# A Trainium2 decoder trunk: the experts' buffers open before the routing, six weight slots come through POOL's queue into h's place, and ten unused products stand on TensorE

## The chip, the cores and the metric

The kernel runs on one core of a Trainium2 chip. The metric is device time in microseconds (us) of one execution; the time of a kernel is the median of its timed runs. One further execution is recorded by the hardware profiler; all rows below come from it.

The engines in the profile are PE (TensorE's products), PEld (its weight loads), DVE (VectorE), ACT (ScalarE), POOL (GpSimd) and SP (SyncE, which here only issues transfers). Each engine runs its instructions in the order in which the program wrote them.

## The reference, cut to what matters

Two layers over 512 tokens of 1024 features. Layer 0 is an mLSTM mixer and a dense SwiGLU, layer 1 an HGRN2 mixer and a top-2-of-8 expert SwiGLU. All inputs are float32.

```python
def rmsnorm(x, w):
    x32 = x.astype(jnp.float32)
    y = x32 * lax.rsqrt(jnp.mean(x32 * x32, axis=-1, keepdims=True) + EPS)
    return (y * w.astype(jnp.float32)).astype(x.dtype)

def swiglu(t, wg, wu, wd):
    return (jax.nn.silu(t @ wg) * (t @ wu)) @ wd

def moe_swiglu(h, router_w, wg, wu, wd):
    ...
    logits = (t @ router_w).astype(jnp.float32)
    top_logits, top_idx = lax.top_k(logits, TOP_K)
    top_w = jax.nn.softmax(top_logits, axis=-1)
    gates = jnp.einsum('tk,tke->te', top_w, jax.nn.one_hot(top_idx, N_EXPERTS, dtype=jnp.float32)).astype(h.dtype)
    for e in range(N_EXPERTS):
        y = y + gates[:, e:e + 1] * swiglu(t, wg[e], wu[e], wd[e])
...
    for layer in range(DEPTH):
        ...
        hn = rmsnorm(x, norm1_w[layer]) * (1 + scale1) + shift1
        y = mlstm_mixer(hn, ...)  or  hgrn2_mixer(hn, ...)
        x = x + gate1 * y
        hn = rmsnorm(x, norm2_w[layer]) * (1 + scale2) + shift2
        y = swiglu(hn, ...)  or  moe_swiglu(hn, ...)
        x = x + gate2 * y
    return rmsnorm(x, final_norm_w)
```

## The kernel before, in words

**Products.** The residual stream is held feature-major: eight tiles `x[k]` of 128 features by 512 tokens. A float32 product is three products of fp32r halves (`hi`, `lo` of the activations, `whi`, `wlo` of the weights: hi by whi, lo by whi, hi by wlo); the experts use two. So every projection is a long row of 128x512 products on PE, k tile by k tile.

**Weights.** All weights are stored as *slots* of 128x1024 float32 (512 KB). The class `Weights` (lines 160 to 255) walks one list, `plan`, of entries of two slots or one. `load` issues an entry's transfer on SP's queue into a buffer of the pool `raw` (two buffers of two slots); `want` lets ACT make `whi` of a slot (a copy to fp32r), `low` lets DVE make `wlo` (the difference). Split slots live in a pool of five and are made three ahead of the one that PE reads. A raw buffer is free when its last `wlo` is made, and only then is the next entry's transfer issued. In the expert phase a second pool, `rawm`, doubles the raw buffers; it is opened after the routing. Its first entries (`raw70`, `raw71`, ...) belong to expert 0. During the start (`ada_first`, line 506), entries 2 and 3 go to a pool `rawf`, and the transfers of the conditioning weights `ad0` to `ad7` (1 MB each) stand between them on SP's queue.

**The norm** (`norm`, line 597). The sum of squares of each token comes from two float32 products `ms<-sq,mean`; ACT turns it into `rs` with two activations; then, for each of eight k tiles, DVE makes `u`, ACT makes `hi` and DVE makes `lo`, and PE runs that tile's products (`group_first`). Of the three norms that go through this function, the first has other work passed in (`before`); the ones ahead of the dense SwiGLU (products `f_in`) and ahead of the HGRN2 projection (products `h_first`) have none.

**Routing and experts.** The last projection of HGRN2 (`h_out`) runs interleaved with `pre_route` (line 1288): residual tiles `xr0` to `xr7` come back from DRAM on POOL's queue, PE makes the logits (`lgt`, `lps`) and transposes of the tokens (`xt`). Then `route` (line 1351) has DVE and ACT work out the two best experts and the place of each token in its expert's list (`mask_b`, `rps`, `pick`), while PE waits. `experts` (line 1563) then takes the eight experts one after the other: PE gathers the expert's tokens into columns (`xT<-pick,xt`, 152 at most), ACT copies them (`xm`), PE makes gate and up products (`gu`), ACT and DVE make `h` (one tile of 2x152 for each of 11 blocks, a buffer each), PE makes the down products (`yd`). Expert e's first three blocks of gate and up (`EARLY`) stand ahead of the down products of expert e-1. What does not fit in an expert's 152 places goes through a branch, `overflow`.

**Names in rows.** A helper records every operation, so that nearly all rows carry its line, L317; the tile names tell them apart. Tiles shown without their number (`raw`, `xr`) stand for all of that name.

Of the kernel before, what the change touches and what calls it, by code (L numbers as in the profile page):

```python
# [152 lines left out]
def moe_order():  # L153

    for e in range(NE + 1):
        if e < NE:
            yield from ((e * MB // 8 + 2 * f, 2) for f in range(EARLY))
        if e:
            base = (e - 1) * MB // 8 + 2 * ET
            yield from ((base + i, min(2, ET - i)) for i in range(0, ET, 2))  # L160
        if e < NE:
            yield from ((e * MB // 8 + 2 * f, 2) for f in range(EARLY, ET))


class Weights:
# [4 lines left out]
    def __init__(self, nc, raw, split, bufs, plan, ahead, loads):  # L170
        self.nc, self.raw, self.split, self.bufs, self.plan = nc, raw, split, bufs, plan
        self.ahead, self.loads, self.early = ahead, loads, {}
# [5 lines left out]
    def load(self, n):  # L178
        while self.next_load < min(n, len(self.plan)):
            src, s0, cnt = self.plan[self.next_load]  # L180
            pool = self.early.get(self.next_load) or self.raw[self.next_load % len(self.raw)]
            t = pool.tile([P, 2, 1024], F32, name=f"raw{self.next_load}", tag="raw")
            self.nc.sync.dma_start(t[:, 0:cnt], src[s0:s0 + cnt].rearrange("s p c -> p s c"))
            for i in range(cnt):
                self.raws[self.loaded] = (t[:, i], self.next_load + (i == cnt - 1))
                self.loaded += 1
            self.next_load += 1

    def want(self, slot):

        nc, left = self.nc, []
        while self.next_slot < min(slot + 1, self.n_slots, self.freed + self.bufs):
            s = self.next_slot
            while s not in self.raws:
                self.load(self.next_load + 1)
# [9 lines left out]
    def low(self, left):  # L205
        for lo, r, hi, i in left:
            self.nc.vector.tensor_sub(lo, r, hi.bitcast(F32))
            self.load(i + 1 + self.loads)
# [179 lines left out]
class Kernel:  # L388
    def __init__(self, nc, tc, ctx, a, dbg):
# [10 lines left out]
        self.W = Weights(nc, [pool("raw", 2)], pool("split", 5), 5, plan, 3, 1)  # L400
# [91 lines left out]


# [12 lines left out]
    def ada_first(self, pool):  # L506
# [22 lines left out]
        for d in range(6):  # L529
            if d % 2 == 0:  # L530
                self.W.load(d // 2 + 1)
            load(d)
        self.W.load(4)
# [63 lines left out]
    def norm(self, l, i, before=()):  # L597
# [3 lines left out]
        for s, t in enumerate(self.ssq):  # L601
            nc.tensor.matmul(ms, self.mean, t, start=s == 0, stop=s == 1)
        rs = self.nrm.tile([P, T], F32, name="rs", tag="rs", bufs=1)
# [114 lines left out]
    def mlstm(self):  # L718
# [3 lines left out]
        with ExitStack() as ctx:  # L722
# [5 lines left out]
            with tc.tile_pool(name="adf", bufs=6) as adf, tc.tile_pool(name="rawf", bufs=2) as rawf:  # L728
                self.W.early = {2: rawf, 3: rawf}
                a0 = self.ada_first(adf)  # L730
# [747 lines left out]
    def moe(self, out, stop):  # L1478
        nc, tc = self.nc, self.tc
        V, S = nc.vector, nc.scalar  # L1480
        with ExitStack() as ctx:
# [9 lines left out]
            nc.gpsimd.memset(self.one_b, 1.0)  # L1491
            lps = self.ps("lps", (P, NC, NE))
# [7 lines left out]
            for _ in self.side:  # L1500
                pass
            pick, rest, *slots = self.route(rp, lps, xt)
            with ExitStack() as ctx:
                pools = [ctx.enter_context(tc.tile_pool(name=n, bufs=2)) for n in ("xe", "he", "wk", "rawm")]
                self.W.raw.append(pools.pop())
                self.W.loads = 3
                g, r, n_over = self.experts(*pools, xt, pick, lambda: rest(*slots))
# [55 lines left out]
    def experts(self, xp, hp, wk, xt, pick, rest):  # L1563
# [4 lines left out]
        xs, hs, ys, rows = {}, {}, {}, {}  # L1568
# [326 lines left out]
```

## Time and profile before

| | |
|---|---|
| time, median of 3 runs | 1565.16 us (1563.8 to 1567.88) |
| time of the profiled execution | 1567.31 us |
| its span in the trace | 1565.5 us |
| PE busy | 1492.9 us, 95% |
| DVE busy | 1088.3 us, 70% |
| ACT busy | 844.6 us, 54% |
| POOL busy | 138.8 us, 9% |
| mean granted TensorE clock | 0.975 |

The profiled execution is 1.8 us longer than its span and 2.15 us above the median of the timed runs. A busy share is a mean over stages: PE is at 99 to 100% in most of them, so its waits stand in few places, and the rows below are from these places. The granted clock is 1.00 at 2.4 GHz and 0.50 at 1.2 GHz; a stretch between has both.

### The profile page before, as it was taken

The numbers are of one execution on the slowest core, as the hardware profiler recorded it, in microseconds if no ns is written. First come the engines' busy times: TensorE is split into PE (matmuls) and PEld (weight loads), VectorE is DVE, ScalarE is ACT, GpSimd is POOL, SyncE is SP. The second block draws the span as 40 slices with busy tenths as digits, with TensorE's granted clock in tenths as the row PEclk, the third lists the DMA queues.
The fourth block names the chain that finished last, engine by engine and source line by source line (L and its number), as shares of the span: only waits on it lengthen the run. The fifth ranks groups of instructions, "written<-read, shape, count | busy, mean of one in ns | idle before, by whom it ended". The sixth has DMA issues, their size and how long they took to land.

```text
span 1565.5 us, 23553 instructions
## 1 busy us (share of the span) xinstructions
PE 1492.9 (95%) x8935; PEld 1312.3 (84%) x8935; DVE 1088.3 (70%) x1991; ACT 844.6 (54%) x1561; POOL 138.8 (9%) x209
## 2 busy tenths in 40 slices
PE   4989999999999999999999998999999999999996
PEld 3867776888888888688888875999999999999994
DVE  6785874655445555585977744787877878788796
ACT  5466433423212322364656543687776868777663
POOL 0041000000000000310000010501010010100061
PEclk8999999999999999999999999999999999999997
DMA  9462551355455553543102132788787887878782
GB/s 375 162 193 77 189 195 60 140 210 188 164 186 184 193 192 118 192 145 108 54 28 81 55 105 108 257 299 302 250 286 269 276 275 260 300 258 272 267 315 91
DMA packets 80854, 300.47 MB, mean 192 GB/s; under 512 B 8036, under 2 KB 8084, under 8 KB 79712
## 3 DMA queue, kind: packets, MB, share of 16 engines
q1 hardware_dynamic: 69424, 266.36, 48.4%
q0 software_dynamic: 11312, 32.56, 6.3%
q8 instruction: 72, 1.18, 0.3%
q14 instruction: 46, 0.38, 0.1%
HBM read 280.78 MB, written 18.09 MB: 191 GB/s over the span
## 4 chain that ended last, share of the span: by engine, by line
PE 84%; DVE 6%; ACT 4%; DMA 4%; issue 1%; POOL 0%; DVEq 0%; SPq 0%; ACTq 0%
PE gu L317 20%; PE yd L317 11%; PE fd L317 8%; PE fgp L317 7%; PE fup L317 7%; PE hh L317 4%; PE al L317 3%; PE hv L317 3%; PE h_out L317 3%; PE m_g L317 3%; PE m_out L317 2%; PE hg L317 2%; PE h_first L317 2%; PE f_in L317 1%; PE o L317 1%; DMA ar<-in_ada 1%
## 5 line engine op out<-in xcount | busy, mean ns | idle before, releaser
L317 DVE TENSOR_TENSOR wlo<-raw,whi 128x1024 fp32r<-128x1024 f32 x403 | 489.8, 1222 | 107.1 <-ACT whi L317 105.0
L317 ACT ACTIVATE whi<-raw 128x1024 fp32r<-128x1024 f32 x403 | 421.9, 1054 | 183.1 <-DMA raw<-in_w 40.3
L317 PE MATMUL gu<-x,whi 128*128 128x304 f32 x1408 | 358.6, 344 | 1.5 <-DVE x L317 1.5
L317 PE MATMUL gu<-x,wlo 128*128 128x152 f32 x1408 | 327.8, 233 | 0.0
L317 PEld LDWEIGHTS gu<-x,wlo 128*128 128x128 f32 x1408 | 269.1, 191 | 0.0
L317 PEld LDWEIGHTS gu<-x,whi 128*128 128x128 f32 x1408 | 264.4, 188 | 1.9 <-DVE x L317 1.9
L317 PE MATMUL yd<-h,whi 128*128 128x304 f32 x704 | 183.2, 348 | 2.7 <-DVE h L317 2.7
L317 PE MATMUL yd<-h,wlo 128*128 128x152 f32 x704 | 164.6, 234 | 0.0
L317 PEld LDWEIGHTS yd<-h,whi 128*128 128x128 f32 x704 | 133.3, 189 | 3.1 <-DVE h L317 3.1
L317 PEld LDWEIGHTS yd<-h,wlo 128*128 128x128 f32 x704 | 135.6, 193 | 0.0
L317 DVE SCALAR_TENSOR_TENSOR ar<-ar,cond 128x1024 f32<-128x1024 f32 x80 | 99.5, 1246 | 3.0 <-DMA ar<-in_ada 2.9
L317 ACT ACTIVATE fhi<-fg 128x512 fp32r<-128x512 f32 x22 | 13.9, 633 | 114.3 <-DVE fg L317 114.3
L317 DVE TENSOR_TENSOR fg<-fg,fup 128x512 f32<-128x512 f32 x20 | 13.8, 688 | 82.6 <-PE fup L317 82.6
L317 PE MATMUL fd<-fhi,whi 128*128 128x512 f32 x176 | 69.6, 396 | 0.0
L317 PE MATMUL fd<-flo,whi 128*128 128x512 f32 x176 | 69.6, 396 | 0.0
L317 PE MATMUL fd<-fhi,wlo 128*128 128x512 f32 x176 | 69.6, 396 | 0.0
L317 ACT ACTIVATE t<-gu 128x152 f32<-128x152 f32 x176 | 47.4, 289 | 32.3 <-PE gu L317 32.3
L317 PE MATMUL fgp<-lo,whi 128*128 128x512 f32 x160 | 62.3, 389 | 0.0
L317 PE MATMUL fgp<-hi,whi 128*128 128x512 f32 x160 | 62.2, 389 | 0.0
L317 PE MATMUL fgp<-hi,wlo 128*128 128x512 f32 x160 | 62.2, 389 | 0.0
L317 PE MATMUL fup<-hi,whi 128*128 128x512 f32 x160 | 62.2, 389 | 0.0
L317 PE MATMUL fup<-lo,whi 128*128 128x512 f32 x160 | 62.2, 389 | 0.0
(407 smaller groups left out, 2996.8 us busy)
## 6 DMA issues: line engine op xcount, KB each, us to landing
raw<-in_moe SPq DMA_DIRECT2D x128, 1024.0 KB, 5.2
raw<-in_w SPq DMA_DIRECT2D x69, 1024.0 KB, 5.0
ar<-in_ada SPq DMA_DIRECT2D x80, 512.0 KB, 4.1
ad<-in_ada SPq DMA_DIRECT2D x8, 1024.0 KB, 17.3
XG<-zero POOLq DMA_DIRECT2D x18, 256.0 KB, 6.4
xr<-XG POOLq DMA_DIRECT2D x28, 152.0 KB, 6.3
raw<-in_moe SPq DMA_DIRECT2D x8, 512.0 KB, 4.0
Y<-yt POOLq DMA_DIRECT2D x14, 256.0 KB, 3.7
```

The source lines that it names most:

```text
L317: r = f(*args, **kw)
```

## The change

Four things are changed.

1. `norm` issues three unused products behind `ms` where it has no other work passed in, that is in two of the norms. They multiply the same two operands as `ms` into a bank that nobody reads.
2. Four of the same products stand between `pre_route` and `route`.
3. The pools of the experts open ahead of `pre_route`, and `rawm` joins the raw pools there. The first six slots of expert 0 become six entries of one slot (`raw70` to `raw75`), are issued on POOL's queue at once, and land in the six buffers `hb` (128x1024 each) that `h` will use later; three tiles of `h` now share one `hb`. The later entries (`raw76` and up) go to `raw` and `rawm` on SP's queue. `load` now issues whenever a raw pool holds fewer than two entries.
4. At the start, entries 2 and 3 are fetched into `rawf` by name, and entry 4 stands ahead of `ad6` and `ad7` on SP's queue.

The diff, cut:

```diff
 def moe_order():
...
-        if e < NE:
+        if e == 0:
+            yield from ((s, 1) for s in range(2 * EARLY))
+        elif e < NE:
             yield from ((e * MB // 8 + 2 * f, 2) for f in range(EARLY))
...
+    def room(self, pool):
+        self.raw.append((pool, []))
+
+    def fetch(self, n, pool, queue, tag="raw"):
+        src, s0, cnt = self.plan[n]
+        t = pool.tile([P, 2 if tag == "raw" else cnt, 1024], F32, name=f"raw{n}", tag=tag,
+                      **({} if tag == "raw" else {"bufs": 2 * EARLY}))
+        queue.dma_start(t[:, 0:cnt], src[s0:s0 + cnt].rearrange("s p c -> p s c"))
+        self.early[n] = t
+
+    def load(self, n, done=0):
+        for _, held in self.raw:
+            held[:] = [x for x in held if x >= done]
         while self.next_load < min(n, len(self.plan)):
-            src, s0, cnt = self.plan[self.next_load]
-            pool = self.early.get(self.next_load) or self.raw[self.next_load % len(self.raw)]
...
+            m = self.next_load
+            if m not in self.early:
+                pools = [x for x in self.raw if len(x[1]) < 2]
+                if not pools:
+                    return
+                pools[0][1].append(m)
+                self.fetch(m, pools[0][0], self.nc.sync)
+            t, cnt = self.early.pop(m), self.plan[m][2]
...
     def low(self, left):
         for lo, r, hi, i in left:
             self.nc.vector.tensor_sub(lo, r, hi.bitcast(F32))
-            self.load(i + 1 + self.loads)
+            self.load(len(self.plan), i)
...
+    def warm(self, n, t):
+        ps = self.ps("warm")
+        for _ in range(n):
+            self.nc.tensor.matmul(ps, self.mean, t, start=True, stop=True)
...
         for d in range(6):
-            if d % 2 == 0:
+            if d == 4:
+                self.W.fetch(2, raw, nc.sync)
+            elif d % 2 == 0:
                 self.W.load(d // 2 + 1)
             load(d)
+        self.W.fetch(3, raw, nc.sync)
         self.W.load(4)
...
             nc.tensor.matmul(ms, self.mean, t, start=s == 0, stop=s == 1)
+        if not before:
+            self.warm(3, self.ssq[0])
         rs = self.nrm.tile([P, T], F32, name="rs", tag="rs", bufs=1)
...
             nc.gpsimd.memset(self.one_b, 1.0)
+            experts = ctx.enter_context(ExitStack())
+            pools = [experts.enter_context(tc.tile_pool(name=n, bufs=2)) for n in ("xe", "he", "wk", "rawm")]
+            self.W.room(pools.pop())
+            for n in range(2 * EARLY):
+                self.W.fetch(self.n_dense + n, pools[1], nc.gpsimd, "hb")
...
+            self.warm(4, self.ssq[0])
             pick, rest, *slots = self.route(rp, lps, xt)
-            with ExitStack() as ctx:
-                pools = [ctx.enter_context(tc.tile_pool(name=n, bufs=2)) for n in ("xe", "he", "wk", "rawm")]
-                self.W.raw.append(pools.pop())
-                self.W.loads = 3
-                g, r, n_over = self.experts(*pools, xt, pick, lambda: rest(*slots))
+            g, r, n_over = self.experts(*pools, xt, pick, lambda: rest(*slots))
+            experts.close()
...
-            h = hs[e, f] = hp.tile([P, 2, CAP], F32R, name=f"h{e}{f}", tag="h", bufs=ET + EARLY + 2)
+            n = e * ET + f
+            if n % 3 == 0:
+                hb[0] = hp.tile([P, 1024], F32R, name=f"hb{n}", tag="hb", bufs=2 * EARLY)
+            h = hs[e, f] = hb[0][:, n % 3 * 2 * CAP:(n % 3 + 1) * 2 * CAP].rearrange("p (s r) -> p s r", s=2)
```

In the changed kernel the helper's line is L337. On PE, at the norm ahead of the dense SwiGLU, stood before (`m_out` is the mLSTM's output projection):

```order
L317 MATMUL m_out_1952<-yhih_1849,wlo_1961 128x512
L317 MATMUL ms<-sq,mean 128x512 x2
L317 MATMUL f_in_2111<-hi_2107,whi_1988 128x512
L317 MATMUL f_in_2111<-lo_2109,whi_1988 128x512
L317 MATMUL f_in_2111<-hi_2107,wlo_1989 128x512
```

and stands now:

```order
L337 MATMUL m_out_1952<-yhih_1849,wlo_1961 128x512
L337 MATMUL ms<-sq,mean 128x512 x2
L337 MATMUL warm<-sq,mean 128x512 x3
L337 MATMUL f_in_2115<-hi_2111,whi_1988 128x512
L337 MATMUL f_in_2115<-lo_2113,whi_1988 128x512
L337 MATMUL f_in_2115<-hi_2111,wlo_1989 128x512
```

Three products have come between the sum of squares and the first product of the projection; ahead of HGRN2 it is the same with `h_first`.

On PE, in the routing, the changed kernel has this between the last transpose of `pre_route` and the first product of `route`; before, the row of `warm` is not there and the rest stands in the same order:

```order
L337 MATMUL xt_7322<-cst_c,xr_7146 128x128
L337 MATMUL warm<-sq,mean 128x512 x4
L337 LDWEIGHTS bef
L337 MATMUL rps<-mask_b,bef 128x32
L337 LDWEIGHTS one_b
L337 MATMUL rps<-mask_b,one_b 128x24
```

The four products stand ahead of `rps`, the product that `route` waits for.

On POOL, ahead of `pre_route`, stood before (`cst_r` and `fw` are constants, `bef` and `one_b` the routing's matrices):

```order
L1261 DMA xr5_7053<-X_83 128x512
L417 DMA cst_r_7073<-in_const_r 128x280
L1486 DMA fw_7075<-in_fnw 128x1024
L1489 CAST bef_7079<-cst_r_7073 128x128
L1491 MEMSET one_b_7081 128x128
L1261 DMA xr6_7088<-X_83 128x512
L1261 DMA xr7_7110<-X_83 128x512
```

and stands now:

```order
L1521 MEMSET one_b_7089 128x128
L189 DMA raw70_7103<-in_moe 128x1024
L189 DMA raw71_7105<-in_moe 128x1024
L189 DMA raw72_7107<-in_moe 128x1024
L189 DMA raw73_7109<-in_moe 128x1024
L189 DMA raw74_7111<-in_moe 128x1024
L189 DMA raw75_7113<-in_moe 128x1024
L1291 DMA xr6_7120<-X_83 128x512
L1291 DMA xr7_7146<-X_83 128x512
```

Six transfers of 512 KB have come ahead of the loads of `xr6` and `xr7`. On SP's queue the entries of the last HGRN2 weights were followed by expert 0's pairs:

```order
L183 DMA raw68_6924<-in_w 128x2x1024
L183 DMA raw69_7032<-in_w 128x1024
L183 DMA raw70_7144<-in_moe 128x2x1024
L183 DMA raw71_7174<-in_moe 128x2x1024
L183 DMA raw72_7273<-in_moe 128x2x1024
L183 DMA raw73_7560<-in_moe 128x2x1024
```

and are followed now by later ones:

```order
L189 DMA raw68_6932<-in_w 128x2x1024
L189 DMA raw69_7040<-in_w 128x1024
L189 DMA raw76_7123<-in_moe 128x2x1024
L189 DMA raw77_7125<-in_moe 128x2x1024
L189 DMA raw78_7180<-in_moe 128x2x1024
L189 DMA raw79_7210<-in_moe 128x2x1024
```

So SP's queue is six slots further on at the same place. At the program's start SP's queue now has `raw4` directly behind `raw3`, ahead of `ad6` and `ad7`; before, it stood directly behind `ad7`.

## Rows read from the trace of the kernel before

**Rows 1.** The page's head and its sections 1 and 4: span; busy time of each engine, share of the span and instructions; the chain that ended last, by engine.

```profile
span 1565.5 us, 23553 instructions
...
PE 1492.9 (95%) x8935; PEld 1312.3 (84%) x8935; DVE 1088.3 (70%) x1991; ACT 844.6 (54%) x1561; POOL 138.8 (9%) x209
...
PE 84%; DVE 6%; ACT 4%; DMA 4%; issue 1%; POOL 0%; DVEq 0%; SPq 0%; ACTq 0%
```

**Rows 2.** Stretches of 2 us at the first of the two norms (the one ahead of the dense SwiGLU): the stretch, its length, busy time and instructions of PE, PEld, DVE, ACT and POOL, granted TensorE clock (1.00 is 2.4 GHz, 0.50 is 1.2 GHz), mean busy share of the DMA engines, GB/s.

```profile
270.00:272.00 2.00, 0.00 (x0) 0.00 (x0) 0.75 (x1) 1.15 (x3) 0.00 (x0) 1.00 0.00 0
272.00:274.00 2.00, 1.30 (x5) 0.86 (x6) 1.61 (x2) 1.31 (x2) 0.00 (x0) 1.00 0.00 0
274.00:276.00 2.00, 2.00 (x6) 1.59 (x5) 1.21 (x3) 0.73 (x1) 0.00 (x0) 0.52 0.31 39
276.00:278.00 2.00, 2.00 (x7) 1.58 (x6) 1.21 (x3) 0.82 (x2) 0.00 (x0) 0.63 0.95 387
```

**Rows 3.** The timeline there: start, length, engine, line, operation and tiles; in square brackets the engine's idle time ahead of it and who ended it. `lo` in the fourth row belongs to the last of eight k tiles.

```profile
268.31 1.12 PE L317 MATMUL ms<-sq,mean 128*128 128x512 f32 x2 [0.33 <-ACT sq L317]
...
272.41 0.50 PE L317 MATMUL f_in<-hi,whi 128*128 128x512 f32 x1 [2.98 <-ACT hi L317]
...
273.20 0.50 PE L317 MATMUL f_in<-lo,whi 128*128 128x512 f32 x1 [0.28 <-DVE lo L317]
...
292.39 0.75 DVE L317 SCALAR_TENSOR_TENSOR lo<-u,mod,hi 128x512 fp32r<-128x512 f32 x1 [0.79 <-ACT hi L317]
...
293.98 0.39 PE L317 MATMUL f_in<-lo,whi 128*128 128x512 f32 x1
```

**Rows 4.** Stretches of 2 us at the second norm (ahead of the HGRN2 projection), columns as in Rows 2.

```profile
640.00:642.00 2.00, 0.15 (x1) 0.00 (x0) 0.43 (x1) 1.32 (x2) 0.00 (x0) 1.00 0.99 363
642.00:644.00 2.00, 0.87 (x2) 0.37 (x2) 1.21 (x3) 1.64 (x2) 0.00 (x0) 0.68 0.31 121
...
648.00:650.00 2.00, 2.00 (x7) 1.60 (x6) 1.34 (x2) 1.57 (x2) 0.00 (x0) 0.62 0.65 266
```

**Rows 5.** The timeline at the second norm, columns as in Rows 3; `lo` is again that of the last k tile.

```profile
639.03 1.12 PE L317 MATMUL ms<-sq,mean 128*128 128x512 f32 x2 [0.71 <-ACT sq L317]
...
643.13 0.80 PE L317 MATMUL h_first<-hi,whi 128*128 128x512 f32 x1 [2.98 <-ACT hi L317]
...
663.10 0.75 DVE L317 SCALAR_TENSOR_TENSOR lo<-u,mod,hi 128x512 fp32r<-128x512 f32 x1 [0.79 <-ACT hi L317]
...
665.73 0.39 PE L317 MATMUL h_first<-lo,whi 128*128 128x512 f32 x1
```

**Rows 6.** Stretches of 0.5 us of PE alone in the routing: the stretch, its length, PE busy time and instructions, granted clock, DMA share, GB/s.

```profile
973.50:974.00 0.50, 0.00 (x0) 0.80 0.00 0
...
984.00:984.50 0.50, 0.50 (x6) 0.96 0.00 0
```

**Rows 7.** The timeline of the routing and of the first gather of expert 0, columns as in Rows 3 (a product of float32 operands is two records).

```profile
972.84 0.63 PE L317 MATMUL xt<-cst_c,xr 128*128 128x128 f32 x4
...
977.75 0.18 PE L317 MATMUL rps<-mask_b,bef 128*128 128x32 bf16 x1 [4.28 <-DVE mask_b L317]
...
978.68 11.15 PE L317 MATMUL xT<-pick,xt 128*128 128x152 f32 x64 [0.68 <-DVE pick L317]
```

**Rows 8.** The chain that ended last, in order of time, in the same place: start, length, engine, tile and line, number of records.

```profile
978.68 9.09 PE xT L317 x48
...
987.80 1.23 ACT xm L317 x3
...
992.29 6.74 PE gu L317 x52
...
1038.49 10.74 PE gu L317 x84
```

**Rows 9.** The timeline at the program's start, PE alone: two products of the same operands as the unused ones, 128x512 in float32, four records.

```profile
14.29 3.78 PE L317 MATMUL ms<-sq,mean 128*128 128x512 f32 x4 [14.29 <-DVE sq L317]
```

**Rows 10.** Who waited for whom on ACT between 985 and 1040 us: in total, times, longest.

```profile
ACT whi L317 <- DMA raw<-in_moe: 6.8, 5, 2.0
```

**Rows 11.** Stretches of the expert phase, columns as in Rows 2.

```profile
1000.00:1030.00 30.00, 30.00 (x248) 30.00 (x247) 25.10 (x53) 20.78 (x45) 8.52 (x14) 1.00 1.02 371
...
1036.00:1038.00 2.00, 1.93 (x16) 1.75 (x15) 1.89 (x6) 2.00 (x5) 0.00 (x0) 1.00 0.50 107
1038.00:1040.00 2.00, 1.51 (x12) 1.51 (x12) 2.00 (x6) 1.79 (x6) 0.00 (x0) 1.00 1.03 422
1040.00:1500.00 460.00, 460.00 (x3741) 459.94 (x3741) 370.80 (x651) 345.60 (x667) 42.62 (x59) 1.00 0.81 275
```

**Rows 12.** The timeline of POOL, ACT and DVE in the last projection of HGRN2, columns as in Rows 3.

```profile
929.26 1.07 POOL L1261 DMA_DIRECT2D xr<-X  x2
...
947.43 2.00 ACT L317 ACTIVATE whi<-raw 128x1024 fp32r<-128x1024 f32 x2 [5.96 <-DMA raw<-in_moe]
...
951.33 0.60 ACT L317 ACTIVATE xt<-xt 128x512 f32<-128x512 f32 x1 [1.90 <-PE xt L317]
...
963.42 0.75 DVE L317 SCALAR_TENSOR_TENSOR xr<-h_out,mod,xr 128x512 f32<-128x512 f32 x1 [0.95 <-PE h_out L317]
```

**Rows 13.** Stretches of 5 us there, columns as in Rows 2.

```profile
925.00:930.00 5.00, 5.00 (x23) 4.13 (x23) 1.11 (x2) 1.58 (x2) 1.74 (x6) 1.00 0.70 274
930.00:935.00 5.00, 5.00 (x23) 4.13 (x22) 0.69 (x2) 0.00 (x0) 0.41 (x2) 1.00 0.33 105
935.00:940.00 5.00, 5.00 (x23) 4.13 (x22) 3.45 (x6) 2.02 (x4) 0.00 (x0) 1.00 0.01 3
940.00:945.00 5.00, 5.00 (x24) 4.14 (x23) 2.96 (x3) 1.46 (x2) 0.00 (x0) 1.00 0.22 70
```

**Rows 14.** The timeline of the program's start: issues of the SP queue, and the first DVE product that reads the last of these loads (the second of its pair follows it).

```profile
21.33 3.82 SPq L519 DMA_DIRECT2D ad<-in_ada  x2
...
25.62 6.17 SPq L183 DMA_DIRECT2D raw<-in_w  x2
...
50.94 1.21 DVE L317 SCALAR_TENSOR_TENSOR ad<-ad,cond 128x1024 f32<-128x1024 f32 x1
```

More of the change, by code (lines that the diff above doesn't have):

```diff
@@ L165, with __init__ @@
 class Weights:
-    def __init__(self, nc, raw, split, bufs, plan, ahead, loads):
-        self.nc, self.raw, self.split, self.bufs, self.plan = nc, raw, split, bufs, plan
-        self.ahead, self.loads, self.early = ahead, loads, {}
+    def __init__(self, nc, raw, split, bufs, plan, ahead):
+        self.nc, self.split, self.bufs, self.plan = nc, split, bufs, plan
+        self.ahead, self.early, self.raw = ahead, {}, []
+        self.room(raw)
         self.freed, self.used, self.left = 0, None, []
@@ L176, in __init__ @@
         self.n_slots = sum(c for _, _, c in plan)
-    def load(self, n):
-        while self.next_load < min(n, len(self.plan)):
-            src, s0, cnt = self.plan[self.next_load]
-            pool = self.early.get(self.next_load) or self.raw[self.next_load % len(self.raw)]
-            t = pool.tile([P, 2, 1024], F32, name=f"raw{self.next_load}", tag="raw")
-            self.nc.sync.dma_start(t[:, 0:cnt], src[s0:s0 + cnt].rearrange("s p c -> p s c"))
+    def room(self, pool):
[9 more added lines that the diff above has]
+            held[:] = [x for x in held if x >= done]
+        while self.next_load < min(n, len(self.plan)):
+            m = self.next_load
[6 more added lines that the diff above has]
+            t, cnt = self.early.pop(m), self.plan[m][2]
             for i in range(cnt):
-                self.raws[self.loaded] = (t[:, i], self.next_load + (i == cnt - 1))
+                self.raws[self.loaded] = (t[:, i], m + (i == cnt - 1))
                 self.loaded += 1
@@ L193, in want @@
             s = self.next_slot
-            while s not in self.raws:
-                self.load(self.next_load + 1)
+            assert s in self.raws
             r, i = self.raws.pop(s)
@@ L399, in __init__ @@
         plan += [(a["moe"], i, n) for i, n in moe_order()]
-        self.W = Weights(nc, [pool("raw", 2)], pool("split", 5), 5, plan, 3, 1)
+        self.W = Weights(nc, pool("raw", 2), pool("split", 5), 5, plan, 3)
         self.dram = pool("dram", 1, space=DRAM)
@@ L504, in bias, with ada_first @@
         return self.V(f"ab{l}").rearrange("p (j d) -> p j d", j=6)[:, j]
-    def ada_first(self, pool):
+    def ada_first(self, pool, raw):
         nc = self.nc
@@ L728, in mlstm @@
             with tc.tile_pool(name="adf", bufs=6) as adf, tc.tile_pool(name="rawf", bufs=2) as rawf:
-                self.W.early = {2: rawf, 3: rawf}
-                a0 = self.ada_first(adf)
+                a0 = self.ada_first(adf, rawf)
                 S.activation(self.cond, self.cond, AF.Silu)
@@ L1567, in experts @@
         R2, HC = CAP - P, CAP // 2
-        xs, hs, ys, rows = {}, {}, {}, {}
+        xs, hs, ys, rows, hb = {}, {}, {}, {}, [None]
         def fetch(e):
```

## The prediction

> **What bounds the kernel now.** I read the page's head first: PE is busy for 1492.9 of 1565.5 us and carries 84% of the chain that ended last [rows 1]. A long stretch of the expert phase has no gap at all, 460.00 us busy of 460.00 [rows 11]. So nothing that another engine does faster counts there; time can be won only where PE waits or where it runs at half clock. Next I read the granted clock in short stretches. At 0.50 PE has half its pace (1.2 instead of 2.4 GHz). Three of the stretches at half clock lie where this change works: behind the first norm (0.52 and 0.63 in the two stretches from 274 to 278) [rows 2], behind the second (0.68 from 642, 0.62 still in 648 to 650) [rows 4], and in the routing, where it falls between 973.5 and 974.0 and is back at 984.0 to 984.5 [rows 6]. Last I read the timeline in each place, to see who supplies PE there. The reader is to see that each fall stands beside a wait of PE: 2.98 us for ACT's first hi at each norm [rows 3, 5], 4.28 us for mask_b in the routing [rows 7].
>
> **The first norm (A).** Added: three products of the kind of ms. One such product (two records) is 1.12 us as the trace has it at full clock [rows 3], about 0.95 when they follow each other, since two of them took 3.78 at half clock, 1.89 each [rows 9]. Three take 2.8 to 3.4. They start where ms ends, 268.31 + 1.12 = 269.43, and end at 272.3 to 272.8; the first f_in product went at 272.41. So they fill the wait, and may be 0 to 0.4 us late. If the clock then stays up, 3.5 us at half (274.0 to 277.5, estimated from the stretches) would give back up to 1.7 us. But the eight k tiles come from DVE and ACT, which do not run faster for it: the last lo starts at 292.39 and takes 0.75, so its product could go at 293.2, a few hundredths behind its end. It went at 293.98; the one of the first tile, at 273.20, had waited 0.28 for its lo, so the pace is DVE's wherever PE is quick. The supply leaves 0.8 us, and hides a late warm product too. **A = 0.8**, ends 0 and 1.7; I take the supply's end, since its row is in this place.
>
> **The second norm (B).** The same three products, from 639.03 + 1.12 = 640.15 to 643.0 to 643.5, against 643.13 before [rows 5]. Half clock lasted from about 642.7 to 649.5 (estimated from the stretches), worth up to 3.4. The last lo starts at 663.10 and takes 0.75, its product could go at 663.9 and went at 665.73. **B = 1.8**, ends 0 and 3.4.
>
> **The routing (C).** xT started at 978.68 and ran at half clock until 984.04; these 5.36 us would be 2.68 at full clock. They lie on the path: the chain goes xT 9.09 us, xm at 987.80, gu at 992.29 [rows 8]. Against it stand the four products, which are ahead of rps. They start when the last xt ends, 972.84 + 0.63 = 973.47, and rps went at 977.75 [rows 7]. All at full clock, 3.8 us, they end at 977.3 and cost nothing. All at half, 7.56 us, they end at 981.0 and rps is 3.3 late. The row says that the clock fell within 0.5 us of the end of the small transposes [rows 6], ahead of any length of waiting, so I expect part of the four to be slow: two at each clock end at 973.47 + 5.68 = 979.15, 1.4 late; if only the first 1.8 are slow, 1.2. With 1.3, **C = 2.68 - 1.3 = 1.4**, ends -0.6 and 2.7.
>
> The Trainium skill, "TensorE: Matmul & The Clock Gate", Part 1, says that half clock is the default state and that activity has to come first to release it. By that rule the four products would be the ones to pay for it, all at half, with C = -0.6. The trace agrees as far as that xT itself ran slow for 5.36 us before the clock came back [rows 6, 7].
>
> **The start of the experts (D).** Between 985 and 1040 ACT waited 6.8 us in five waits for raw entries [rows 10], the DMA engines were full for 30 us at 371 GB/s, and PE lost 0.07 + 0.49 us in 1036 to 1040 [rows 11], ahead of the gu group at 1038.49 [rows 8]. Now six slots land before the routing, and four pairs follow in raw and rawm, 14 slots against four before. This wait goes. **D = 0.6**, ends 0 and 0.8 (a quicker stretch of gu products by then). What is late next is PE itself, since it is full from there on.
>
> **Edits that I cost at nothing.** Six fetches on POOL stand ahead of xr6 and xr7: an issue is 1.07 / 2 = 0.54 us [rows 12], so the two come 3.2 us later, issued near 932.5. The first reader that matters, DVE's xr, runs at 963.42 [rows 12]; 20 us of cover or more. The fetches and the first two pairs are 5.2 MB; at 371 GB/s some 14 us, from 929 to 943, when the DMA share was 0.33 and 0.01 [rows 13]. The engine that waits for them is ACT, in order, for the first whi; before, it waited for the same weights until 947.43, and what stands behind it, xt at 951.33, waited for PE anyway [rows 12]. Packing h adds no instruction, and frees a buffer by threes. At the start raw4 (1 MB, 2.8 us at 371 GB/s) delays ad6 and ad7 by about that; their issues began at 21.33 and the last DVE product that needs them ran at 50.94 [rows 14], with 2 MB to land in between. If this cover were thin, it would cost up to 2.8.
>
> **The sum.** A + B + C + D = 0.8 + 1.8 + 1.4 + 0.6 = 4.6. Against the profiled execution that is 1567.3 - 4.6 = 1562.7. The median of the timed runs is 1565.16, which gives 1560.6. Timed runs lie 4.1 us apart, as much as my sum; a run that was shorter may have had less half clock to win back. I therefore take a little less than the whole sum: **1561.2**, a gain of 4.0.
>
> **Rivals.**
>
> *More comes back.* All four routing products run at full clock (C = 2.7), and at the first norm the projection gains more than the supply bound (A up to 1.7, since DVE and ACT also split weights there that wait for buffers which PE frees). Sum 5.9 to 6.8: about 1558.8. For it: PE comes to the routing from a projection at clock 1.00 [rows 13]. Against: the clock fell within 0.5 us of PE's last transpose, so it was not the long wait that brought it down.
>
> *Less comes back.* Either the unused products do not hold the clock in the norms, and only C + D = 2.0 is left, 1563.2 (that the change does not do what it says); or the four in the routing run at half throughout, A + B + C + D = 2.6, 1562.6. For the second: xT ran at half for 5.36 us while PE was working. Against the first: nothing in PE waits is left there for a fall to stand beside.
>
> *Slower: ACT is held by the fetches.* The whi of raw70 is queued on ACT ahead of xt (951.33), on which the routing depends. If raw70 lands after 951.3, all behind it on ACT moves, and PE with it. Eating the sum takes a landing after 951.3 + 4.6 = 955.9, and slower by 0.3% after 960.6: then about 1570. From 932.5 that is 28 us for 5.2 MB, under 190 GB/s, where the trace has 371 at full share [rows 11] and idle engines just there [rows 13]; and raw70 is the first of the six.
>
> The Trainium skill, "Trainium Kernel Development and Optimization", Key Constraints, says that transfers of SP's, ACT's and POOL's queues share 16 DMA engines and interleave. So a second queue would buy order and issue time, no bandwidth. No row of before has both queues full at once.
>
> **How the numbers follow.** About 0.3% (4.7 us) is what a measurement of this kernel can tell from no change; the border lies at 1560.5. My forecast, chance 0.60, sits beside it: 0.25 on the faster side, 0.35 within. More comes back: 0.20, all faster. Less: 0.15, all within (0.08 for the first kind, 0.07 for the second). Slower: 0.05. That makes 0.45 faster, 0.50 within 0.3%, 0.05 slower. The range: down to 1557.4 (below the second case by its A and B ends), up to 1563.6 (just above the third case); what is left out is the slow case, the far ends of B and C, and an unseen spread of the median.
>
> **What the changed profile would show.** Right: clock 1.00 through both norms, and PE's lo products right behind the last lo (A, B); xT at 1.00 from its first product, 64 records in some 8.5 us instead of 11.15, with rps 1 to 1.5 us behind its mask_b (C); raw70 to raw75 landing between 930 and 942, no ACT wait for raw after 985, and no PE gap in the 1036 to 1040 group (D). Wrong: a fall of the clock behind 272 or 643 in spite of the products; xT at 0.50 again, or warm products that end past 980; ACT idle at the first whi of expert 0 beyond xt's time.

## The result, and the profile after

| | before | after |
|---|---|---|
| median | 1565.6 us (5 runs, 1563.8 to 1569.3) | 1557.27 us (5 runs, 1554.15 to 1558.81) |
| profiled execution | 1567.31 us | 1557.43 us |
| its span | 1565.5 us | 1555.7 us |

The ratio of the runs is 0.9928, with a 95% interval of 0.9909 to 0.9948: faster by 8.3 us, where 4.0 was forecast, and just under the low end of the range (1557.4). The page of the changed kernel, head, busy time and chain, against [rows 1]:

```profile
span 1555.7 us, 23596 instructions
...
PE 1492.9 (96%) x8955; PEld 1306.8 (84%) x8955; DVE 1089.2 (70%) x1991; ACT 845.3 (54%) x1561; POOL 133.3 (9%) x215
...
PE 86%; DVE 7%; ACT 3%; DMA 2%; issue 2%; DVEq 0%; SPq 0%; ACTq 0%
```

PE is busy for as long as before, though it has twenty records more (ten unused products): what they add, the higher clock takes away.

The first norm, in stretches of 2 us with the columns of [rows 2]:

```profile
268.00:270.00 2.00, 1.60 (x5) 0.45 (x3) 1.04 (x2) 1.18 (x3) 0.00 (x0) 1.00 0.00 0
270.00:272.00 2.00, 1.71 (x7) 1.24 (x7) 2.00 (x3) 0.63 (x1) 0.00 (x0) 1.00 0.00 0
272.00:274.00 2.00, 1.71 (x8) 1.08 (x7) 1.21 (x3) 0.72 (x1) 0.00 (x0) 1.00 0.45 115
```

and in its timeline, against [rows 3] (the fifth row is the `lo` of the last k tile):

```profile
265.63 1.13 PE L337 MATMUL ms<-sq,mean 128*128 128x512 f32 x2 [0.33 <-ACT sq L337]
266.59 2.74 PE L337 MATMUL warm<-sq,mean 128*128 128x512 f32 x6
269.74 0.50 PE L337 MATMUL f_in<-hi,whi 128*128 128x512 f32 x1 [0.40 <-ACT hi L337]
...
270.52 0.50 PE L337 MATMUL f_in<-lo,whi 128*128 128x512 f32 x1 [0.29 <-DVE lo L337]
...
289.70 0.75 DVE L337 SCALAR_TENSOR_TENSOR lo<-u,mod,hi 128x512 fp32r<-128x512 f32 x1 [0.80 <-ACT hi L337]
...
290.54 0.47 PE L337 MATMUL f_in<-lo,whi 128*128 128x512 f32 x1
```

The reader is to see three things. The granted clock stays at 1.00. The wait of 2.98 us is down to 0.40. And the last lo product starts 0.84 us behind the start of its lo (290.54 against 289.70), where it stood 1.59 behind it before: PE now follows DVE. The second norm, against [rows 5], is the same:

```profile
636.65 2.74 PE L337 MATMUL warm<-sq,mean 128*128 128x512 f32 x6
639.80 0.49 PE L337 MATMUL h_first<-hi,whi 128*128 128x512 f32 x1 [0.40 <-ACT hi L337]
...
659.77 0.75 DVE L337 SCALAR_TENSOR_TENSOR lo<-u,mod,hi 128x512 fp32r<-128x512 f32 x1 [0.79 <-ACT hi L337]
...
660.60 0.47 PE L337 MATMUL h_first<-lo,whi 128*128 128x512 f32 x1
```

and its clock, with the columns of [rows 4], stays up too:

```profile
640.00:642.00 2.00, 1.71 (x7) 1.19 (x7) 2.00 (x3) 0.69 (x1) 0.00 (x0) 1.00 0.00 0
```

The routing, against [rows 7], and then PE's stretches in it (PE busy, clock, DMA share, GB/s):

```profile
967.59 0.98 PE L337 MATMUL xt<-cst_c,xr 128*128 128x128 f32 x4
968.37 4.97 PE L337 MATMUL warm<-sq,mean 128*128 128x512 f32 x8
973.18 0.18 PE L337 MATMUL rps<-mask_b,bef 128*128 128x32 bf16 x1
...
974.20 8.50 PE L337 MATMUL xT<-pick,xt 128*128 128x152 f32 x64 [0.77 <-DVE pick L337]
```

```profile
968.00:970.00 2.00, 2.00 (x5) 0.50 0.00 0
970.00:972.00 2.00, 2.00 (x5) 0.72 0.00 0
972.00:974.00 2.00, 1.42 (x8) 1.00 0.00 0
974.00:976.00 2.00, 1.80 (x14) 1.00 0.00 0
```

The first of the four products pay for the low clock, and the clock is back before xT, which takes 8.50 us in place of 11.15. That was forecast to the tenth (11.15 - 2.68 = 8.5).

**Where the difference lies.** PE's order is the same in both kernels but for the ten products, so the start of the first product of each part can be set side by side. This table is worked out from such starts in all seventeen profiles of the study (us; "first norm" is from the first f_in product to the first fgp product behind it (fgp is the gate product of the dense SwiGLU's third block), "second norm" from h_first to the first ad product of HGRN2, "routing" from the end of the last xt product to the first yd product of expert 0, "experts" from there to la, the first of the last products ahead of the output):

| profile | start to f_in | first norm | second norm | routing | experts |
|---|---|---|---|---|---|
| before, as shown | 272.4 | 24.06 | 32.33 | 75.60 | 493.8 |
| e1, e13: before | 270.5, 268.6 | 24.10, 24.05 | 32.33, 32.12 | 75.50, 84.05 | 490.4, 494.7 |
| after | 269.7 | 23.40 | 30.64 | 74.32 | 490.6 |
| e4, e5: after | 266.0, 269.9 | 23.38, 23.41 | 30.64, 30.65 | 74.38, 76.63 | 491.1, 491.6 |
| e12, e14: after | 269.5, 271.3 | 23.41, 23.39 | 30.63, 30.61 | 76.53, 77.82 | 490.6, 494.5 |
| e2: no products | 271.9 | 24.10 | 32.34 | 74.78 | 490.8 |
| e3: products only | 266.3 | 23.42 | 30.62 | 77.24 | 495.0 |
| e6: norms only | 267.4 | 23.40 | 30.65 | 74.75 | 492.0 |
| e7: routing only | 271.2 | 24.06 | 32.34 | 76.50 | 490.3 |
| e8: half the scatters | 268.4 | 23.41 | 30.65 | 72.92 | 490.7 |
| e9: new order | 269.0 | 23.38 | 30.61 | 72.66 | 494.9 |
| e10: new order, three | 270.1 | 23.41 | 30.65 | 71.81 | 492.9 |
| e11: new order, no four | 268.6 | 23.39 | 30.61 | 74.74 | 490.4 |
| e15: with a tail product | 266.7 | 23.39 | 30.62 | 76.88 | 490.2 |

The two norms are sharp to 0.1 us (but 32.12 in e13): 0.66 and 1.69 us come from the products, whatever the execution. The routing takes a few values, which the experiments explain. The first and the last column scatter by 6.4 and 4.8 us; no product was added there but one in e15's last column. These two are not untouched: part 4 of the change works in the first, and part 3 in the last. The last column follows the clock: in the six profiles with 492.9 us or more the clock falls once near its end, beside waits of PE for h, and in the other eleven it does not. Three of the six are among the four profiles with the old buffers (before, e13, e3), three among the thirteen with the new ones (e9, e10, e14). Of the 9.8 us between the two spans shown, the norms and the routing carry 0.66 + 1.69 + 1.28 = 3.6; 2.7 lie ahead of the first norm, 3.2 behind the first yd product, and 0.2 in the rest.

### The profile page after: what moved, and what is told of

The parts are those of the page before. It is cut to its first block, busy times and chain, and to the rows that moved or that the text cites. A ratio compares the mean times of both kernels' runs of the same rounds, so it can differ in the third digit from the quotient of the medians.

```text
span 1555.7 us, 23596 instructions
## 1 busy us (share of the span) xinstructions
PE 1492.9 (96%) x8955; PEld 1306.8 (84%) x8955; DVE 1089.2 (70%) x1991; ACT 845.3 (54%) x1561; POOL 133.3 (9%) x215
## 4 chain that ended last, share of the span: by engine, by line
PE 86%; DVE 7%; ACT 3%; DMA 2%; issue 2%; DVEq 0%; SPq 0%; ACTq 0%
PE gu L337 21%; PE yd L337 11%; PE fd L337 8%; PE fgp L337 7%; PE fup L337 7%; PE hh L337 4%; PE al L337 3%; PE hv L337 3%; PE h_out L337 3%; PE m_g L337 3%; PE m_out L337 2%; PE hg L337 2%; PE o L337 2%; PE v L337 1%; PE f_in L337 1%
## 5 line engine op out<-in xcount | busy, mean ns | idle before, releaser
L337 DVE TENSOR_TENSOR wlo<-raw,whi 128x1024 fp32r<-128x1024 f32 x403 | 489.7, 1222 | 101.7 <-ACT whi L337 99.8
L337 ACT ACTIVATE whi<-raw 128x1024 fp32r<-128x1024 f32 x403 | 422.1, 1055 | 169.0 <-DMA raw<-in_w 35.9
L337 PE MATMUL gu<-x,whi 128*128 128x304 f32 x1408 | 358.7, 344 | 1.4 <-DVE x L337 1.0
L337 PE MATMUL gu<-x,wlo 128*128 128x152 f32 x1408 | 327.8, 233 | 0.6 <-issue 0.6
L337 PEld LDWEIGHTS gu<-x,wlo 128*128 128x128 f32 x1408 | 269.1, 191 | 0.7 <-issue 0.4
L337 PEld LDWEIGHTS gu<-x,whi 128*128 128x128 f32 x1408 | 264.4, 188 | 1.9 <-DVE x L337 1.1
L337 PE MATMUL yd<-hb,whi 128*128 128x304 f32 x704 | 181.4, 346 | 1.3 <-DVE hb L337 1.3
L337 PE MATMUL yd<-hb,wlo 128*128 128x152 f32 x704 | 164.2, 233 | 0.0
L337 PEld LDWEIGHTS yd<-hb,wlo 128*128 128x128 f32 x704 | 134.6, 191 | 0.0
L337 PEld LDWEIGHTS yd<-hb,whi 128*128 128x128 f32 x704 | 132.3, 188 | 1.5 <-DVE hb L337 1.5
L337 DVE SCALAR_TENSOR_TENSOR ar<-ar,cond 128x1024 f32<-128x1024 f32 x80 | 98.7, 1237 | 2.8 <-DMA ar<-in_ada 2.7
L337 ACT ACTIVATE fhi<-fg 128x512 fp32r<-128x512 f32 x22 | 13.9, 633 | 114.3 <-DVE fg L337 114.3
L337 DVE TENSOR_TENSOR fg<-fg,fup 128x512 f32<-128x512 f32 x20 | 13.8, 688 | 82.7 <-PE fup L337 82.7
L337 PE MATMUL fd<-fhi,whi 128*128 128x512 f32 x176 | 69.6, 396 | 0.0
L337 PE MATMUL fd<-flo,whi 128*128 128x512 f32 x176 | 69.6, 396 | 0.0
L337 PE MATMUL fd<-fhi,wlo 128*128 128x512 f32 x176 | 69.6, 396 | 0.0
L337 ACT ACTIVATE t<-gu 128x152 f32<-128x152 f32 x176 | 48.2, 289 | 35.9 <-PE gu L337 34.3
L337 PE MATMUL fgp<-lo,whi 128*128 128x512 f32 x160 | 62.3, 389 | 0.0
L337 PE MATMUL fgp<-hi,whi 128*128 128x512 f32 x160 | 62.2, 389 | 0.0
L337 PE MATMUL fgp<-hi,wlo 128*128 128x512 f32 x160 | 62.2, 389 | 0.0
L337 PE MATMUL fup<-hi,whi 128*128 128x512 f32 x160 | 62.2, 389 | 0.0
L337 PE MATMUL fup<-lo,whi 128*128 128x512 f32 x160 | 62.2, 389 | 0.0
```

Of the source, the lines that this page charges most:

```text
L337: r = f(*args, **kw)
```

## The experiments

Every group below ran on one chip, beside its own runs of the kernel before, and five comparisons of the same two kernels came of it:

| | before, median | after, median | ratio, 95% interval |
|---|---|---|---|
| first | 1565.6 (5 runs) | 1557.27 (5) | 0.9928 (0.9909 to 0.9948) |
| e4 | 1561.85 (35) | 1558.8 (12) | 0.9979 (0.9964 to 0.9994) |
| e5 | 1562.59 (35) | 1559.53 (12) | 0.9989 (0.9975 to 1.0003) |
| e12 | 1563.28 (32) | 1559.98 (12) | 0.9987 (0.9971 to 1.0002) |
| e14 | 1569.2 (28) | 1562.62 (12) | 0.9943 (0.9919 to 0.9966) |

The intervals of e5 and e12 just include no change; those of the other three do not.

### Group 1: the parts, and both kernels again (e1 to e4)

**e1**, the kernel before unchanged. 

> The kernel before once more, for a second profile. Theory one (the surplus is the kernel's): the profile has again what the changed kernel lacked outside the forecast terms, that is gathers yg of 27 us in sum on POOL against 20, a last group of down products that waits some 1.3 us longer for h and a fall of the clock near 1520 that costs 1.7. Theory two (the surplus is the profiled execution's): one or more of these are gone, and the profile of this kernel differs from the first by 1 to 3 us at places that no edit touches. Median 1565 to 1567 by both.

Measured 1561.87 us, ratio 0.9996 (0.9981 to 1.0011). The profile has its gathers yg (of the experts' rows at the end) in 19.6 us, no fall of the clock near 1520, and 490.4 us in the experts' column in place of 493.8. So this kernel has no long end in every execution. It can have one: e3 and e13, which have the old buffers too, show it again.

**e2**, the changed kernel without the products:

```diff
-        if not before:
-            self.warm(3, self.ssq[0])
...
-            self.warm(4, self.ssq[0])
```

> The changed kernel without its ten unused products; early buffers, POOL's fetches and the start stay. If the products are worth the forecast A + B + C = 4.0 and the rest of the change the other 4 to 5 us: 1561 to 1562. If the products alone carry the gain of 8 to 9: 1565 to 1566. If the buffers carry it: 1557 to 1558. The clock falls again behind both norms and in the routing.

Measured 1559.98, ratio 0.9984 (0.9970 to 0.9997). The routing column falls by 0.7 against e1, the forecast's D (0.6): PE's gap at 1036 is gone. The median is 1.9 us below the kernel before (0.5 to 4.7 by the interval), so that more than D may have come back without any product; one profile does not show where.

**e3**, the opposite: the kernel before with `warm` and its two calls. 

> The kernel before with the ten unused products and nothing else. By the forecast terms 1565.6 - 4.0 = 1561.6. If the products carry the whole gain: 1557. If the surplus belongs to the buffers: not under 1561. In the profile the clock stays at 1.00 behind both norms, and the end of the expert phase looks as in the kernel before (sum of the yg gathers 27 us) if the buffers are its cause.

Measured 1561.16, ratio 1.0002 (0.9988 to 1.0016): no gain that is clear of the noise, where 4.0 was forecast. Both norms have their gain, and the routing column is the longest of the group, 77.24. PE ran xT quickly and then stood 2.51 us for the tokens of the second gather, and the clock fell behind that (1014.7 to 1018.1).

**e4**, the changed kernel again. 

> The changed kernel once more, for a second profile beside the others on one chip. 1556 to 1558. Theory one: yg gathers of 20 us in sum again, no fall of the clock near 1513. Theory two: the end looks as in the kernel before, or the 0.7 us that PE lost at 1001 to 1003 is gone.

Measured 1558.8, 3.1 below the kernel before. PE waits 1.24 us at the same place, and the clock does not fall there.

### Group 2: what takes the routing's gain (e5 to e8)

**e5**, the changed kernel unchanged. 

> The changed kernel for the third time, to anchor the others of this group and to settle its size. If the first comparison (8.3 us) was large by the draw of executions: 3 to 5 us below the kernel before. If 8 to 9 us is the size and the second comparison (3.1) was small: 7 to 9 below.

Measured 3.1 us below, as in group 1. POOL's timeline, from the last of sixteen scatters of tokens (into XG, a tensor in DRAM with the tokens sorted by expert) to the loads of the second gather, which read XG:

```profile
1000.91 1.50 POOL L1453 DMA_INDIRECT XG<-zt,put  x1 [0.22 <-issue]
1002.40 0.97 POOL L1485 DMA_DIRECT2D GM<-gt  x1
1003.95 0.60 POOL L1611 DMA_DIRECT2D xr<-XG  x1 [0.57 <-issue]
1009.64 1.56 POOL L1611 DMA_DIRECT2D xr<-XG  x3 [5.09 <-issue]
```

PE's timeline at the transposes of these tokens, and its stretches there (columns as above):

```profile
1016.12 0.23 PE L337 MATMUL xT<-cst_c,xr 76*128 76x76 f32 x1
1018.71 0.75 PE L337 MATMUL xT<-cst_c,xr 76*128 76x76 f32 x5 [2.36 <-DMA xr<-XG]
```

```profile
1018.00:1020.00 2.00, 1.29 (x8) 0.73 1.03 372
1020.00:1022.00 2.00, 2.00 (x10) 0.50 1.02 410
```

Three of the four loads are issued only from 1009.64 on, after POOL's queue has stood for 5.09 us behind the first; the four land 6.6 to 8.8 us after their issue. What the queue stands for, this row does not say ("issue"); that it is the scatters, e8 and e9 test. PE is there too early by 2.36 us, and then the clock falls.

**e6**, only the four products of the routing taken out of the changed kernel:

```diff
-            self.warm(4, self.ssq[0])
```

> The changed kernel without the four products of the routing; those of the two norms stay. By the forecast (C = 1.4): 1.4 us above the changed kernel. If POOL's chain of scatters to the second gather is what comes next (it showed a PE wait of 1.24 us at the first transposes of xr in the last profile), xT at half clock is partly hidden by that wait and the four are worth under 1 us: the wait is gone here, and the time is 0 to 1 us above. Rival: 2.6, the whole of xT's half clock.

Measured 1558.48, 1.05 us below e5; ratio to before 0.9980 (0.9965 to 0.9996). xT is slow again, and the wait for xr is gone:

```profile
968.80 0.19 PE L337 MATMUL rps<-mask_b,bef 128*128 128x32 bf16 x1 [4.29 <-DVE mask_b L337]
...
969.72 11.11 PE L337 MATMUL xT<-pick,xt 128*128 128x152 f32 x64 [0.68 <-DVE pick L337]
```

So the four are worth nothing here, or less than nothing: the routing column is 74.75 without them and 76.63 with them (e5).

**e7**, only the six of the norms taken out (the first two lines of e2's diff). 

> The changed kernel without the six products of the two norms; the four in the routing stay. By the forecast A + B = 2.6 us above the changed kernel, with the clock at half behind both norms in the profile and full clock in xT. Rival: the products of the norms give nothing that lasts (the time won is waited for later): no more than 0.5 above.

Measured 1564.5, ratio 1.0020 (1.0005 to 1.0035): slower than before. The columns of the norms are those of before, and the routing is 76.50, with a wait of 1.77 for xr and a fall of the clock. The norms account for 2.3 of the 5 us above e5; the two profiles lie only 2.3 apart in all, so that they do not show the rest.

**e8**, half the scatters left out, so that the upper half of the features of experts 1 to 7 is zero:

```diff
-                for j in range(2):
+                for j in range(1):
                     for c in range(2):
                         nc.gpsimd.memset(spacer, 0.0)
```

> The changed kernel with eight of the sixteen scatters XG of the routing left out (the upper half of the features of every expert but the first stays zero), so that POOL's chain ahead of the second gather is some 10 us shorter. If that chain holds PE at the first transposes of xr: no PE wait there, and 0.7 to 1.3 us below the changed kernel. If it does not: the same time within 0.5 us.

Measured 1554.02, 5.5 us below e5; ratio to before 0.9964 (0.9951 to 0.9977). No PE wait for xr, and the routing takes 72.92, 3.7 less than in e5. POOL's chain is what took the gain; the other 1.8 us of the median are not in this column.

### Group 3: another order of the scatters (e9 to e12)

**e9**, nothing left out:

```diff
-            for i in range(NC):
-                for j in range(2):
+            for j in range(2):
+                for i in range(NC):
                     for c in range(2):
...
-            for q in range(2):
-                r0 = e * CAP + q * HC
-                for j in range(2):
+            for j in range(2):
+                for q in range(2):
+                    r0 = e * CAP + q * HC
                     nc.gpsimd.dma_start(rows[e][q][j], self.XG[j][r0:r0 + HC])
```

> The changed kernel with the sixteen scatters and the four loads of each gather in another order: the lower half of the features first for all token tiles, then the upper. Nothing is left out. If PE waits at the first transposes of xr because the loads stand behind the last scatter: that wait of 1.2 to 2.5 us and the fall of the clock behind it go, and the time is 1.8 to 3 us below the changed kernel, about that of the half scatter less some tenths. Rival: the chain's end still holds the second half's transposes, and no more than 0.7 us comes back.

Measured 1556.61, ratio to before 0.9957 (0.9941 to 0.9973), 3.4 us below e12. POOL's timeline now has both loads that the first transposes read at once, and PE does not wait for xr:

```profile
1001.61 0.97 POOL L1485 DMA_DIRECT2D GM<-gt  x1
1002.58 1.15 POOL L1611 DMA_DIRECT2D xr<-XG  x2
1008.93 1.04 POOL L1611 DMA_DIRECT2D xr<-XG  x2 [5.21 <-issue]
```

**e10**, e9 with `self.warm(3, ...)` in the routing. 

> As the one before, with three products in the routing in place of four. The four made rps 0.3 to 0.7 us late. If three end ahead of mask_b and still keep the clock through xT: 0.3 to 0.7 us less than with four. Rival: the clock falls again in xT in some executions, and it is 0.5 to 1.5 us more.

Measured 1556.1, ratio 0.9958 (0.9942 to 0.9974). The routing takes 71.81 against 72.66, a little more than forecast (0.3 to 0.7); the medians, 0.5 apart, cannot tell it from no change.

**e11**, e9 without the four. 

> The new order of the scatters without the four products of the routing. If the order matters only because a quicker xT makes PE arrive too early, it is worth nothing here: the same time as norms only (some 4 us below the kernel before), and 1.5 to 2 us above the new order with the products. Rival: the order is worth something by itself, and this is as quick as the other.

Measured 1558.24, ratio 0.9975 (0.9961 to 0.9989), 1.6 us above e9. The routing takes 74.74, as in e6: the order alone is worth nothing, and the four alone are not either; together they are worth 2.1.

**e12**, the changed kernel unchanged. 

> The changed kernel for the fourth time, as the anchor of this group. By the second and third comparison 2 to 4 us below the kernel before; by the first 8 to 9.

Measured 3.3 below the kernel before.

### Group 4: is the surplus the draw? (e13 to e15)

**e13**, the kernel before unchanged. 

> The kernel before for a third profile. In the profiles so far the stretches that the change does not touch (start to the first f_in product, first down product to the last group) were 266 to 272 and 490 to 495 us long in kernels of either kind. If they scatter by execution: this profile lies anywhere in these ranges, with the first norm at 24.1 us, the second at 32.3 and the routing to the first down product at 75.5. If the long ones belong to the kernel before: 270 to 272 and 494 again.

Measured 1572.36, and 1569.2 in the group's own runs of it (1560.09 to 1579.78): on this chip the kernel before is 6 to 10 us slower than on the three others. The norms are where they were. The routing takes 84.05, which I had not expected by either theory. ACT's and PE's timelines, and the stretch:

```profile
984.95 0.58 ACT L317 ACTIVATE x<-xm 128x456 fp32r<-128x456 f32 x1
989.81 0.85 ACT L317 ACTIVATE xm<-xT,mod,A 128x152 f32<-128x152 f32 x2 [4.28 <-remote]
```

```profile
991.71 0.62 PE L317 MATMUL gu<-x,whi 128*128 128x304 f32 x1 [4.47 <-DVE x L317]
```

```profile
985.00:1000.00 15.00, 10.53 (x65) 10.35 (x64) 5.97 (x7) 4.98 (x8) 12.81 (x21) 0.77 0.65 229
```

ACT stands 4.28 us ahead of the copy of the last part of xT, for something that the trace does not show ("remote": no instruction in the profile released it). That copy is on PE's path: PE waits 4.47, and the clock has a mean of 0.77 in these 15 us.

**e14**, the changed kernel unchanged. 

> The changed kernel for the fifth time. Draw of executions: 2 to 4 us below the kernel before, the first norm 23.4, the second 30.6, routing to the first down product 74.3 or 76.5 (with a fall of the clock behind the wait for xr). If the first comparison was the edit's size on some chips: 8 to 9 below on one more chip.

Measured 6.6 below the kernel before. ACT stands as long here, but 13 us later, ahead of an instruction of the first block of gate and up:

```profile
998.51 0.30 ACT L337 ACTIVATE t<-gu 128x152 f32<-128x152 f32 x1
1002.95 0.30 ACT L337 ACTIVATE t<-gu 128x152 f32<-128x152 f32 x1 [4.14 <-remote]
```

It costs PE less there: its waits beside the pause are 0.68 and less each, though the clock falls behind them, and the routing column is 77.82, 6.2 under e13. The changed kernel's first profile has pauses of the same kind in the same place, which no profile of groups 1 to 3 has. The row is from who waited for whom on ACT (total, times, longest):

```profile
ACT whi L337 <- remote: 1.6, 1, 1.6
ACT t L337 <- remote: 1.4, 1, 1.4
```

**e15**, e10 with one more unused product ahead of the last h of the last expert's first down group:

```diff
                 for f in range(ET):
+                    if (e, i, f) == (NE - 1, 0, ET - 1):
+                        self.warm(1, self.ssq[0])
```

> The reordered scatters with three products in the routing, and one more unused product ahead of the last h of the last expert's first down group, where PE waits 1.3 us in every profile and the clock fell behind that wait in three of fourteen. If that wait is what makes the end scatter: the stretch from the first to the last down group is 490 to 491 us, and the time is 0 to 1 us below the version without it. If the scatter comes from DVE's late gathers: 490 to 495 as before, and the same time.

Measured 1557.02, ratio 0.9947 (0.9918 to 0.9976), 5.6 below e14. No PE wait is left at that place and the experts' column is the shortest of all, 490.2. One profile does not show that it stays there: e1, e7 and e11 have 490.3 to 490.4 without the product. The routing took 76.88, with a pause of ACT of 4.31 us as in e14, and e10, with 71.81, did not run on this chip. Two counts in what was expected are off: the clock had fallen at that place in four of the fourteen profiles so far (before, e3, e9, e10), and the wait of 1.3 us was not in every one (1.02 in e1, 1.07 in e7, 1.74 in the first).

## Why the prediction was wrong

**The norms (A, B): right.** Forecast 0.8 and 1.8, measured 0.66 and 1.69 between the two profiles shown, and within 0.1 us of it wherever the products stand or are left out (but for 32.12 in e13). Bounding the gain by the supply of lo, and not by the length of the half clock (1.7 and 3.4), was the step that made it.

**The start of the experts (D): right.** Forecast 0.6, measured 0.7 (e2 against e1).

**The routing (C): the gain was there and was spent.** From rps to the first gu product PE needed 11.85 us before (e1) and 9.26 after, 2.6 saved. The four products ran for 4.97 us and delayed rps by 0.2 to 0.7, not by the 1.3 of the forecast, so that 1.9 to 2.4 were left where 1.4 was forecast. (The forecast read half clock off [rows 9]; the granted clock reads 1.00 there, so it rests on the duration alone. At 1.00 three of the products took 2.74 us, 0.91 each, near the 0.95 that it took.) What failed is the sentence "What is late next is PE itself": next is the second gather, behind POOL's sixteen scatters (e5, e8, e9). Against the kernels without the four (74.7), C is 1.8 to 2.1 without the wait (e8, e9); with it 0.4 (e4) or -1.8 to -1.9 (e5, e12), by whether the clock falls there. I looked for what follows the first gather on PE, and not for the queue that feeds the next one, which the same routing starts.

**The sum: the step that failed.** A + B + C + D was forecast at 4.6, and the three columns measured 3.6 between the two profiles shown: 0.66, 1.69 and 1.28, the last for C and D together, where 2.0 was forecast. The other 6.2 of the 9.8 us lie where the prediction put nothing: 2.7 ahead of the first norm, where it saw only a possible cost, 3.2 in the experts ("it is full from there on"), and 0.2 in the rest. The range was built from sums of the four terms, and "an unseen spread of the median" was left out of it, though the timed runs lay "4.1 us apart, as much as my sum". The runs show a spread larger than that sum: 266.0 to 272.4 us ahead of the first norm, 490.2 to 495.0 in the experts, and 6 to 11 us between the runs of one kernel on three of the chips. Only the stretches at half clock "where this change works" were priced. One more stood near the end of the experts in the profile before, and none in the profile after. First PE's wait for h there and the clock beside it, before:

```profile
1518.97 0.41 PE L317 MATMUL yd<-h,whi 128*128 128x304 f32 x1 [1.74 <-DVE h L317]
```

```profile
1518.00:1520.00 2.00, 1.03 (x8) 1.03 (x9) 2.00 (x4) 2.00 (x3) 0.40 (x1) 0.98 1.02 404
1520.00:1522.00 2.00, 2.00 (x11) 2.00 (x10) 2.00 (x3) 1.86 (x3) 0.00 (x0) 0.50 0.66 250
```

and the clock behind the same wait after (columns of [rows 2]):

```profile
1512.00:1514.00 2.00, 2.00 (x19) 2.00 (x18) 2.00 (x3) 2.00 (x4) 0.00 (x0) 1.00 0.28 111
```

The other comparisons give 3.1, 3.1 and 3.3 (e4, e5, e12), near the 4.0 forecast, and 6.6 (e14). That nearness is in part luck: in the one profile each of e5 and e12 the three columns add up to 1.2 and 1.4 against e1, since C was lost there.

**What stays open.** Whether the first 8.3 are a draw of executions, that chip, or in part the new buffers. For the draw: 6.2 of the 9.8 us between the two profiles lie in stretches that vary as widely in kernels of either kind. For the buffers: a long end stands in three of four profiles with the old ones and in three of thirteen with the new, and e2's median lies 1.9 lower where its routing gives 0.7. These are too few to show it. The new order of the queues at the start shows nothing of the kind (266.3 to 272.4 in the four profiles without it, 266.0 to 271.9 in the thirteen with it). For the chip: on the fourth the change is worth 6.6. In the one profile of each kernel there, ACT's pause falls on PE's path before and mostly beside it after, and the first profile after has shorter pauses of that kind. Its counterpart of before has none. What holds ACT in them, and whether the change moves them, no run here shows.

**The rivals.** The first comparison lies nearest to "More comes back" (1558.8), but not by its mechanism: A stayed at 0.66, and the four products did not all run at full clock. "Less comes back" named two causes, and neither happened: the clock held in the norms, and the four were at half for a part only. Less did come back in the routing, by the second gather, which no rival named. ACT was not held by the fetches (the slower rival): the splits that waited 5.96 us for expert 0's weights before [rows 12] follow without a wait at 935.17 in the first profile after, and no ACT wait for raw was left behind 985.

## What to carry to other kernels

A stretch that is made faster hands its gain to whatever feeds the next one: follow each queue that the same event starts (here POOL's scatters, 24 us long) to the first reader, before the gain is counted. Keep PE busy through a wait where what comes after it is limited by PE, and count the gain only up to the supply. Where runs of one kernel scatter by more than the effect, compare the parts that the edit touches, product by product, in several profiles: here that told 0.7 us apart, where the interval of a comparison of 12 with 35 runs is 4 to 5 us wide.

The best kernels of the study are the changed one with the scatters in the new order (e9, e10): 0.9957 and 0.9958 of the kernel before, and 0.9947 with the tail product (e15) on the chip where the kernel before was slowest.

## What was not expected of the hardware

The granted clock falls behind a single PE wait of 1.77 us (e7, at 1023.8), and in e14, near 1003, behind five of 0.24 to 0.68 that lie within 5 us. It does not fall behind one of 1.24 (e4). Near the end of the experts it falls beside waits of 1.21 and 1.30 in e9 and not beside 1.26 and 1.30 in e6, whose products there are the same: that column is 494.9 us in the one and 492.0 in the other. And on one chip of four ACT stood still for 4.1 to 4.3 us at the start of the experts with no cause in the trace, in three profiles out of three.
